# First-phase scaling of four projection jobs from SBUF, order pins for weight sums and statistics, and a later broadcast, in a fp32 decoder-block kernel

## The chip, the cores and the metric

The kernel runs on one core of a Trainium2 chip. The metric is the device time of one execution in microseconds (us), the median of several runs. TensorE (PE in the profile) multiplies matrices, VectorE (DVE) and ScalarE (ACT) work elementwise, GpSimd (POOL) does some elementwise work and issues DMAs, and SyncE (SP) issues DMAs.

## The reference

One layer over 2048 prompt tokens and 64 sample tokens, in fp32:

```
z = rms_norm(x, pre_g)
xr, gr, u, v, gs = split(z @ w_in)            # 1024 columns each
xc = causal_depthwise_conv(xr, buf, conv_w)   # 4 taps
hr = rg_lru(xc, sigmoid gates from w_r, w_i)  # recurrence along the tokens
br = hr * silu(gr)
bs = chunk_spatial_gating(gelu(u), rms_norm(gelu(v), sgu_g)) * silu(gs)
out = concat(br, bs) @ w_out
y = x + rms_norm(out, post_g)
```

rms_norm divides a token's row by the root of its mean square and multiplies by a gain for each channel.

## The kernel before, in words

**Groups and phases.** The tokens are cut into four groups of 512 prompt tokens; group 0 also takes the 64 sample tokens (T0 = 576 columns, two halves of 288). Phase one does group 0, and there a scheduler with priorities orders each engine's instructions. Phase two does groups 1 to 3 with Strassen-like products in steps, in the order in which the code is written (`manual_schedule`). Products keep fp32 precision by three matmuls, high times high, high times low and low times high.

**Weights.** A weight piece of 128x1024 is loaded by an SP DMA (`wraw`), ScalarE rounds it to a high half (`wh`, L187), VectorE subtracts that for the low half (`wl`, L195), and TensorE uses both. The work is prepared three pieces ahead, and a `wh` buffer comes free when TensorE has finished the piece three before.

**Jobs of phase one.** Jobs are 128 columns of w_in or w_out: xr0, xr1, gr8, gr9, xr2, xr3, gr10, gr11 and so on, then v, then gs, gs, u, u four times, then 16 out jobs. Here f0 to f3 are the first four. All but the v jobs have two pieces, 96 matmuls of 128x288 in all, and leave their result in two PSUM banks. The pool for them has six banks, so a job needs the banks of the job three before it. The matmuls run on x times gain. The division by the row norm comes after: `scaled` (L397) multiplies the two banks by rsB, a 128x576 tile with each token's factor. It is made by `norm_a` (`row_rstd`, L264: matmuls nsA and nsB sum the squares, VectorE takes the root's reciprocal) and `norm_b` (`row_bcast`, L289: VectorE builds the diagonal dg, matmuls nsC and nsD spread it over the partitions, VectorE copies it out). The same pair with the name "o" serves the norm after the out jobs, early in phase two (steps 4 and 10 of it), and `finish0` scales, adds and stores the 16 blocks of the result of group 0.

**Side work.** `make_sums` (L239) prepares weight sums for phase two: for each of 16 c-units (pairs of columns of w_in) POOL's queue loads four quadrants (B11, B12, B22, B21), VectorE adds four times, and POOL's queue stores the sums. For 12 more units (w_v, w_or) GpSimd does the adds. `stat_sum` and `z_norm` prepare group 1 during the out jobs. `later` keeps an instruction at its place in the program where the scheduler would otherwise issue it earlier by priority.

**Gates.** The xr jobs are scaled and convolved (`conv`, xc), split into xch and xcl, and multiplied with gate weights on TensorE (two spare banks), then go through sigmoids on ScalarE and a scan on VectorE. The first gate matmuls come behind the fifth job.

Of the kernel before, what the change touches and what calls it, by code (L numbers as in the profile page):

```python
# [11 lines left out]
AF = mybir.ActivationFunctionType  # L12
ALU = mybir.AluOpType
# [27 lines left out]
C_PRE, C_POST, C_CW, C_CB, C_BR, C_BI, C_LAM, C_SG = 0, 16, 32, 64, 72, 80, 88, 96  # L41
# [13 lines left out]
def hybrid_layer(ctx: ExitStack, tc: tile.TileContext, a):  # L55
    nc = tc.nc
# [15 lines left out]
    def blk(name, dt=F32):  # L72
        return bp.tile([P, T0 + 3], dt, tag="blk", name=name)
# [70 lines left out]
    state = {}  # L144
# [94 lines left out]
    def make_sums(unit):  # L239
        nm = "_".join(str(x) for x in unit)  # L240
        t = state.pop(("quad", unit))

        def put(k, x):
            sums[unit, k] = hp.tile([P, W], F32, name=f"{k}_{nm}")
            side.dma_start(sums[unit, k], x)

        eng = nc.vector if unit[0] == "c" else nc.gpsimd
        eng.tensor_add(t["B11"], t["B11"], t["B12"])
        put("P1", t["B11"])
        eng.tensor_add(t["B12"], t["B12"], t["B22"])  # L250
        put("P3", t["B12"])
        eng.tensor_add(t["B22"], t["B22"], t["B11"])
        put("P2", t["B22"])
        eng.tensor_add(t["B21"], t["B21"], t["B22"])
        put("P4", t["B21"])
# [98 lines left out]
    def banks(job):  # L354
        if ("ps", job) not in state:
            n = NC0 if is_v(job) else 2
            state["ps", job] = [bank(f"gm0{job[0]}{job[1]}_{o}") for o in range(n)]
        return state["ps", job]
# [35 lines left out]
    def cm_banks(job):  # L394
        return [(p[:, :n], o, n) for p, (o, n) in zip(banks(job), halves0)]

    def scaled(job, dst):  # L397
        rb = state["rxB"]
        for p, o, n in cm_banks(job):
            nc.vector.tensor_mul(dst[:, o:o + n], p, rb[:, o:o + n])  # L400

# [221 lines left out]
    def stat_sum(g, n):  # L623
        c, b = divmod(n, 2)
        if n == 0:
            state["xss", g] = mp.tile([P, 4, 2], F32, tag="xss", name=f"xss{g}")
        x = state.pop(("xs", g, n))
        nc.scalar.activation(x, x, AF.Square, accum_out=state["xss", g][:, c, b:b + 1])

    def stat_rstd(g):  # L630
        sv = mp.tile([P, 4], F32, tag="xsv", name=f"xsv{g}")
# [21 lines left out]
    def z_norm(g, j, rows=(0, 1)):  # L653
        x = state["R", g, j]
        for i in rows:
            nc.vector.scalar_tensor_tensor(x[:, i, :TP], x[:, i, :TP], col(C_PRE, 2 * j + i), state["rB", g],
                                           op0=ALU.mult, op1=ALU.mult)

    def parts(key, j):
        lo, hi = state[(*key, j)], state.get((*key, 4 + j))  # L660
# [84 lines left out]
    early, tasks, late = defaultdict(list), defaultdict(list), defaultdict(list)  # L745

    def at2(s, f, *args):

        tasks[s].append((f, *args))
# [300 lines left out]
    jobs = []  # L1050
# [8 lines left out]
    for job in jobs:  # L1059
        kind, j = job  # L1060
# [9 lines left out]
    for s in steps:  # L1070
        for job, i in s:
            kind, j = job
# [30 lines left out]
    handlers = {"xr": on_xr, "gr": on_silu, "gs": on_silu, "v": on_v0, "u": on_u0, "out": on_out0}  # L1103
    mid = {}
    plan = {job: [(handlers[job[0]], job)] for job in jobs}
# [1 line left out]
    def at(job, f, *args):  # L1107
        plan[job].append((f, *args))

    f0, f1, f2 = jobs[:3]  # L1110
    plan[f0], plan[f1] = [], []
    plan[f2] = [(norm_a, "x")]
    mid[jobs[3]] = [(norm_b, "x")] + [(handlers[f[0]], f) for f in (f0, f1, f2)] + [(gate_in0, 0), (gate_in0, 1)]
    for hp_ in range(0, NH, 2):
        i = jobs.index(("gr", NH + hp_ + 1))
        if hp_ == 0:
# [26 lines left out]
    for j in range(8):  # L1143
        at(("out", 8 + j // 2), z_raw, 1, j)
        at(("out", 11 + j // 3), z_norm, 1, j)
# [58 lines left out]
    for g in range(1, NG):  # L1204
        G = len(steps2)
        V, U, O, R2 = G + 56, G + 84, G + 140, G + 168
# [22 lines left out]
        wide(g, "v", "w_v", 0, put_v(g))  # L1229
        if g == 1:  # L1230
            for j in range(KT):
                t = 12 + 2 * j if j < 8 else V + 3 + 2 * (j - 8)
                at2(t, finish0_load, j)
                t += 3
                at2(t, finish0_scale, j)
                at2(t + 1, finish0_add, j)
                at2(t + 4, finish0_store, j)
        else:
            at2(G - 1, load_gq, g - 1, 1)
            for n in range(4):  # L1240
                k = (g - 1, (1, 1, 0, 0)[n], (3, 2, 2, 3)[n])
                t = G + (5, 7, 9, 11)[n]
                at2(t, finish_scale, *k)
                at2(t + 1, finish_add, *k)
                at2(t + 6, finish_store, *k)
            at2(V + 16, load_gq, g - 1, 0)
            for n in range(4):
                k = (g - 1, n % 2, n // 2)
                t = V + 21 + 3 * n
                at2(t - 5, finish_load, *k)  # L1250
                at2(t, finish_scale, *k)
                at2(t + 1, finish_add, *k)
                at2(t + 6, finish_store, *k)
# [70 lines left out]
    at2(R2 + 28, last_rstd, 0)  # L1324
    for qq in range(4):
        at2(R2 + 29, last_both, 0, qq)
    late[4].append((norm_a, "o"))
    late[10].append((norm_b, "o"))

    base = pos_of[steps2[0][3]]  # L1330
    with tc.manual_schedule():
# [84 lines left out]
```

## Time and profile before

| | |
|---|---|
| median of 3 runs | 2570.75 us (2570.57 to 2571.52) |
| profiled execution | 2568.9 us |
| its span | 2567.1 us |
| TensorE busy | 2497.7 us, 97% of the span |
| VectorE, ScalarE, POOL busy | 68%, 54%, 18% |
| mean granted TensorE clock | 0.991 of full speed |

The profile is of one execution, and 1.8 us of its time lie outside the span. A row of the timeline names an instruction and, in brackets, how long its engine had been idle before it and which instruction ended that. Line numbers in rows are those of the kernel before.

### The profile page before, as it was taken

What the parts mean: (1) busy time and instruction counts of PE and PEld (TensorE: products, weight loads), DVE (VectorE), ACT (ScalarE), POOL (GpSimd) and SP (SyncE); (2) the same over time, 40 slices, a digit from 0 to 9 for tenths busy, and PEclk for the clock granted to TensorE, in tenths of its full rate; (3) what the DMA queues carried; (4) which work ended last, traced back from release to release, by engine and by line L of the source; (5) the groups of instructions that cost most, each with busy time, mean ns of one, the idle gap of its engine ahead of it and who ended that gap; (6) DMA issues with size and microseconds to landing.
All of it is one profiled execution on the core that took longest, in us unless ns stands there. A gap on an engine that the chain in (4) does not pass through costs nothing.

```text
span 2567.1 us, 41558 instructions
## 1 busy us (share of the span) xinstructions
PE 2497.7 (97%) x16710; PEld 2300.2 (90%) x16710; DVE 1748.8 (68%) x2244; ACT 1391.6 (54%) x1777; POOL 470.5 (18%) x548
## 2 busy tenths in 40 slices
PE   7989999999999999999999999999999999999997
PEld 6989789999999998799878998799878998799886
DVE  7776155545466686756888686756888687756866
ACT  5444342223324577545756677545756577645654
POOL 4331024964751201100100100100000100100000
PEclk9999999999999999999999999999999999999999
DMA  6995389985964766756776755855776755855576
GB/s 226 332 328 214 107 286 322 369 276 193 323 221 155 228 210 207 233 182 187 268 260 197 239 192 180 252 178 186 258 274 197 240 177 185 254 192 181 187 253 198
DMA packets 167649, 587.11 MB, mean 229 GB/s; under 512 B 19216, under 2 KB 19776, under 8 KB 167456
## 3 DMA queue, kind: packets, MB, share of 16 engines
q1 hardware_dynamic: 107184, 378.11, 44.5%
q0 software_dynamic: 59696, 205.30, 24.0%
q8 instruction: 130, 2.13, 0.3%
q10 hardware_dynamic: 576, 1.05, 0.1%
q14 instruction: 63, 0.52, 0.1%
HBM read 494.92 MB, written 89.47 MB: 228 GB/s over the span
## 4 chain that ended last, share of the span: by engine, by line
PE 77%; DMA 7%; DVE 7%; ACT 5%; issue 3%; POOL 1%; SPq 0%; DVEq 0%; ACTq 0%; POOLq 0%
PE gm0out L370 8%; PE gm0v L381 4%; PE gm0gs L370 4%; PE gm0u L370 4%; PE gm0gr L370 3%; DMA wraw_c_P<-P_c 2%; PE gm0xr L370 2%; DVE wl_c_B L195 1%; DMA wraw_c_B<-w_in 1%; PE g L862 1%; PE sp L559 1%; PE w2o1a L716 1%; PE w2o1d L716 1%; PE w3o0d L716 1%; PE w1o1a L716 1%
## 5 line engine op out<-in xcount | busy, mean ns | idle before, releaser
L187 ACT ACTIVATE wh_c_P<-wraw_c_P 128x1024 fp32r<-128x1024 f32 x192 | 203.0, 1059 | 255.4 <-DMA wraw_c_P<-P_c 73.8
L195 DVE TENSOR_TENSOR wl_c_P<-wraw_c_P,wh_c_P 128x1024 fp32r<-128x1024 f32 x192 | 234.3, 1221 | 105.4 <-ACT wh_c_P L187 103.2
L195 DVE TENSOR_TENSOR wl_c_B<-wraw_c_B,wh_c_B 128x1024 fp32r<-128x1024 f32 x144 | 175.4, 1221 | 86.0 <-ACT wh_c_B L187 85.9
L187 ACT ACTIVATE wh_c_B<-wraw_c_B 128x1024 fp32r<-128x1024 f32 x144 | 152.2, 1058 | 147.6 <-DMA wraw_c_B<-w_in 24.8
L187 ACT ACTIVATE wh_w_or_P<-wraw_w_or_P 128x1024 fp32r<-128x1024 f32 x96 | 101.6, 1058 | 83.9 <-DMA wraw_w_or_P<-P_w_or 27.7
L195 DVE TENSOR_TENSOR wl_w_or_P<-wraw_w_or_P,wh_w_or_P 128x1024 fp32r<-128x1024 f32 x96 | 117.4, 1223 | 40.9 <-ACT wh_w_or_P L187 40.4
L187 ACT ACTIVATE wh_w_or_B<-wraw_w_or_B 128x1024 fp32r<-128x1024 f32 x72 | 76.1, 1059 | 79.6 <-DMA wraw_w_or_B<-w_or 15.8
L370 PE MATMUL gm0out<-c0l,wh_out 128*128 128x288 f32 x512 | 110.5, 297 | 1.0 <-DVE c0l L161 0.8
L370 PE MATMUL gm0out<-c0h,wh_out 128*128 128x288 f32 x512 | 110.7, 297 | 0.0
L370 PE MATMUL gm0out<-c0h,wl_out 128*128 128x288 f32 x512 | 110.1, 296 | 0.0
L195 DVE TENSOR_TENSOR wl_w_or_B<-wraw_w_or_B,wh_w_or_B 128x1024 fp32r<-128x1024 f32 x72 | 87.9, 1221 | 30.0 <-ACT wh_w_or_B L187 29.5
L195 DVE TENSOR_TENSOR wl_out<-wraw_out,wh_out 128x1024 fp32r<-128x1024 f32 x32 | 53.0, 1657 | 54.0 <-ACT wh_out L187 53.9
L620 POOL DMA_DIRECT2D xs<-xt x24 | 12.9, 538 | 391.5 <-PE sp L559 291.9
L370 PEld LDWEIGHTS gm0out<-c0l,wh_out 128*128 128x128 f32 x512 | 82.0, 188 | 1.6 <-DVE c0l L161 1.4
L431 POOL DMA_DIRECT2D wg<-w_g x16 | 11.9, 743 | 387.9 <-ACT xch L846 128.9
L370 PEld LDWEIGHTS gm0out<-c0h,wh_out 128*128 128x128 f32 x512 | 82.0, 188 | 0.6 <-issue 0.5
L370 PEld LDWEIGHTS gm0out<-c0h,wl_out 128*128 128x128 f32 x512 | 82.2, 188 | 0.0
L187 ACT ACTIVATE wh_out<-wraw_out 128x1024 fp32r<-128x1024 f32 x32 | 33.8, 1056 | 83.4 <-PE gm0out L370 51.6
L195 DVE TENSOR_TENSOR wl_w_v_P<-wraw_w_v_P,wh_w_v_P 128x1024 fp32r<-128x1024 f32 x48 | 58.5, 1221 | 29.6 <-ACT wh_w_v_P L187 29.6
L187 ACT ACTIVATE wh_w_v_P<-wraw_w_v_P 128x1024 fp32r<-128x1024 f32 x48 | 50.0, 1054 | 48.7 <-DMA wraw_w_v_P<-P_w_v 32.7
L370 PE MATMUL gm0gr<-z0h,wl_gr 128*128 128x288 f32 x256 | 57.3, 305 | 8.3 <-DVE wl_gr L195 8.3
L370 PE MATMUL gm0xr<-z0h,wh_xr 128*128 128x288 f32 x256 | 56.6, 303 | 7.2 <-ACT wh_xr L187 5.4
(1609 smaller groups left out, 8660.9 us busy)
## 6 DMA issues: line engine op xcount, KB each, us to landing
wraw_c_P<-P_c SPq DMA_DIRECT2D x192, 512.0 KB, 4.2
wraw_c_B<-w_in SPq DMA_DIRECT2D x144, 512.0 KB, 4.3
wraw_w_or_P<-P_w_or SPq DMA_DIRECT2D x96, 512.0 KB, 4.3
wraw_w_or_B<-w_or SPq DMA_DIRECT2D x72, 512.0 KB, 3.8
wraw_w_v_P<-P_w_v SPq DMA_DIRECT2D x48, 512.0 KB, 3.6
wraw_w_v_B<-w_v SPq DMA_DIRECT2D x36, 512.0 KB, 3.5
wraw_out<-w_out SPq DMA_DIRECT2D x32, 512.0 KB, 4.5
xs<-xt POOLq DMA_DIRECT2D x24, 512.0 KB, 5.8
```

Of the source, the lines that this page charges most:

```text
L187: nc.scalar.activation(h[:, sl], raw[:, sl], AF.Copy)
L195: nc.vector.tensor_sub(l[:, sl], raw[:, sl], h[:, sl].bitcast(F32))
L370: nc.tensor.matmul(p[:, :n], w, zz[:, o:o + n], start=(k == 0 and n_pass == 0), stop=(k == KT - 1 and n_pass == 2))
L381: nc.tensor.matmul(p[:n], zz[:, c * P:c * P + n], w, start=(k == 0 and n_pass == 0), stop=(k == KT - 1 and n_pass == 2))
L431: side.dma_start(w2.rearrange("p (h c) -> p h c", h=2), a["w_g"][hp_:hp_ + 2].rearrange("h p a c -> p h (a c)"))
L559: nc.tensor.matmul(p[:, c * P:(c + 1) * P], state["vn", c, h // 4][:, vs], wst[:, h, :], start=True, stop=True)
L620: side.dma_start(x, a[f"xt{g}"][c * P:(c + 1) * P, b * W:(b + 1) * W])
L716: nc.tensor.matmul(bks[b], zz, w, start=(not cont and kk == 0 and n_pass == 0), stop=(kk == HALF - 1 and n_pass == 2), skip_group_check=True)
L862: nc.tensor.matmul(p, ww[:, ws], xx[:, i, :TP], start=n_pass == 0, stop=n_pass == 2)
```

## The change

The first add of each c-unit, the squares of group 1's statistic and the first row of each of its `z_norm` blocks are pinned with `later`. A function `raw_out` copies both banks of f0 to f3 to an SBUF tile, and `scaled` multiplies that tile by rsB in one instruction of 576 columns. `norm_b("x")` moves from behind f3's first piece in the program to behind its second. `norm_a("o")` and `norm_b("o")` move from behind steps 4 and 10 of phase two to behind steps 8 and 14, and the `finish0` blocks shift: seven blocks from step 14 on, then the other nine from one step behind the start of the v products on.

```diff
@@ make_sums
-        eng.tensor_add(t["B11"], t["B11"], t["B12"])
+        i = eng.tensor_add(t["B11"], t["B11"], t["B12"])
+        if unit[0] == "c":
+            later(i)
@@
+    def raw_out(job):
+
+        t = state["rawp", job] = blk(f"raw0{job[0]}{job[1]}")
+        for p, o, n in cm_banks(job):
+            nc.vector.tensor_copy(t[:, o:o + n], p)
+
     def scaled(job, dst):
         rb = state["rxB"]
+        if ("rawp", job) in state:
+            nc.vector.tensor_mul(dst[:, :T0], state.pop(("rawp", job))[:, :T0], rb)
+            return
         for p, o, n in cm_banks(job):
             nc.vector.tensor_mul(dst[:, o:o + n], p, rb[:, o:o + n])
@@ stat_sum
-        nc.scalar.activation(x, x, AF.Square, accum_out=state["xss", g][:, c, b:b + 1])
+        i = nc.scalar.activation(x, x, AF.Square, accum_out=state["xss", g][:, c, b:b + 1])
+        if g == 1:
+            later(i)
@@ z_norm
+            if g == 1 and i == 0:
+                later(n)
@@
-    f0, f1, f2 = jobs[:3]
-    plan[f0], plan[f1] = [], []
-    plan[f2] = [(norm_a, "x")]
-    mid[jobs[3]] = [(norm_b, "x")] + [(handlers[f[0]], f) for f in (f0, f1, f2)] + [(gate_in0, 0), (gate_in0, 1)]
+    f0, f1, f2, f3 = jobs[:4]
+    plan[f0], plan[f1] = [], [(raw_out, f0), (raw_out, f1)]
+    plan[f2] = [(norm_a, "x"), (raw_out, f2)]
+    plan[f3] = ([(raw_out, f3), (norm_b, "x")] + [(handlers[f[0]], f) for f in (f0, f1, f2)]
+                + [(gate_in0, 0), (gate_in0, 1)] + plan[f3])
@@ finish0, the steps of phase two
-                t = 12 + 2 * j if j < 8 else V + 3 + 2 * (j - 8)
+                t = 14 + 2 * j if j < 7 else V + 1 + 2 * (j - 7)
@@
-    late[4].append((norm_a, "o"))
-    late[10].append((norm_b, "o"))
+    late[8].append((norm_a, "o"))
+    late[14].append((norm_b, "o"))
```

TensorE's order at the norm of x, in the kernel before (gm0gr_..._533 is f2, gm0gr_..._664 is f3):

```order
L370 MATMUL gm0gr_0_533<-z0h_271,wl_gr_1_477 128x288
L370 MATMUL gm0gr_1_534<-z0h_271,wl_gr_1_477 128x288
L272 MATMUL nsAx_641<-accx_121,ones 128x512
L276 MATMUL nsBx_644<-accx_121,ones 64x64
L296 MATMUL nsCx_715<-dgx_640,ones 128x512
L302 MATMUL nsDx_719<-dgx_640,ones 128x64
L370 MATMUL gm0gr_0_664<-z0h_117,wh_gr_0_529 128x288
L370 MATMUL gm0gr_0_664<-z0l_118,wh_gr_0_529 128x288
```

The same place in the changed kernel (gm0gr_0_673 is f3):

```order
L372 MATMUL gm0gr_1_540<-z0h_271,wl_gr_1_477 128x288
L274 MATMUL nsAx_647<-accx_121,ones 128x512
L278 MATMUL nsBx_650<-accx_121,ones 64x64
L372 MATMUL gm0gr_0_673<-z0h_117,wh_gr_0_535 128x288
L372 MATMUL gm0gr_1_674<-z0h_117,wh_gr_0_535 128x288
```

Here nsC and nsD no longer stand behind nsA and nsB. They stand behind the last matmul of f3, ahead of the fifth job (gm0xr_0_856):

```order
L372 MATMUL gm0gr_1_674<-z0l_272,wh_gr_1_591 128x288
L372 MATMUL gm0gr_0_673<-z0h_271,wl_gr_1_593 128x288
L372 MATMUL gm0gr_1_674<-z0h_271,wl_gr_1_593 128x288
L298 MATMUL nsCx_781<-dgx_646,ones 128x512
L304 MATMUL nsDx_785<-dgx_646,ones 128x64
L372 MATMUL gm0xr_0_856<-z0h_117,wh_xr_0_669 128x288
L372 MATMUL gm0xr_1_857<-z0h_117,wh_xr_0_669 128x288
```

So nsC and nsD have moved past all 96 matmuls of f3. On VectorE, in the first recurrence (heads 0 and 1: r, a and q are its factors), the order before is:

```order
L484 SCALAR_TENSOR_TENSOR r_0_952<-q_0_1168,r_0_952 128x576
L490 MEMSET a_0_1162 128x1
L497 MEMSET a_0_1162 128x8
L248 TENSOR_TENSOR pB11c_0_1900<-pB11c_0_1900,pB12c_0_1902 128x1024
L484 SCALAR_TENSOR_TENSOR r_1_974<-q_1_1172,r_1_974 128x576
L490 MEMSET a_1_1165 128x1
L497 MEMSET a_1_1165 128x8
L250 TENSOR_TENSOR pB12c_0_1902<-pB12c_0_1902,pB22c_0_1904 128x1024
L489 MEMSET r_0_952 128x1
L489 MEMSET r_1_974 128x1
L252 TENSOR_TENSOR pB22c_0_1904<-pB22c_0_1904,pB11c_0_1900 128x1024
L491 TENSOR_TENSOR i_0_963<-i_0_963,r_0_952 128x576
```

and in the changed kernel:

```order
L495 SCALAR_TENSOR_TENSOR r_0_960<-q_0_1176,r_0_960 128x576
L501 MEMSET a_0_1170 128x1
L508 MEMSET a_0_1170 128x8
L495 SCALAR_TENSOR_TENSOR r_1_982<-q_1_1180,r_1_982 128x576
L501 MEMSET a_1_1173 128x1
L508 MEMSET a_1_1173 128x8
L500 MEMSET r_0_960 128x1
L502 TENSOR_TENSOR i_0_971<-i_0_971,r_0_960 128x576
L500 MEMSET r_1_982 128x1
L507 TENSOR_TENSOR i_0_971<-i_0_971,ah_1189 128x8
L509 SCALAR_TENSOR_TENSOR xc_0_791<-a_0_1170,i_0_971 128x512
```

The adds of a c-unit (pB11c, pB12c, pB22c), which stood between the factors of the two heads, are gone from this stretch, and the next `wl_gr` stands 15 rows behind the first of the two r instead of 23. The second recurrence, heads 2 and 3, has lost its first adds in the same way. The adds come later: of the 16 units six instead of ten begin ahead of the v jobs, and the last one begins some 20 VectorE rows later among the gs and u jobs.

## Rows read from the trace of the kernel before

**Rows 1.** The page's first part: busy time of each engine, its share of the span, its instructions.

```profile
PE 2497.7 (97%) x16710; PEld 2300.2 (90%) x16710; DVE 1748.8 (68%) x2244; ACT 1391.6 (54%) x1777; POOL 470.5 (18%) x548
```

**Rows 2.** TensorE's waits, grouped (what waited, for whom, total us, times, longest us).

```profile
PE gm0gr L370 <- DVE wl_gr L195: 8.3, 2, 4.8
...
PE nsCx L296 <- DVE dgx L294: 5.2, 1, 5.2
...
PE nsCo L296 <- DVE dgo L294: 2.5, 1, 2.5
```

**Rows 3.** Timeline of TensorE over the statistics of the first norm and the fourth job. Columns here and in the other timelines: start us, duration us, engine, line, operation, out<-in, count, and in brackets the idle time just before and what ended it.

```profile
56.45 1.02 PE L272 MATMUL nsAx<-accx,ones 128*128 128x512 f32 x2
57.40 0.33 PE L276 MATMUL nsBx<-accx,ones 128*64 128x64 f32 x2
62.98 2.05 PE L296 MATMUL nsCx<-dgx,ones 128*128 128x512 f32 x2 [5.25 <-DVE dgx L294]
...
66.62 0.58 PE L370 MATMUL gm0gr<-z0h,wh_gr 128*128 128x288 f32 x1 [0.98 <-DVE xr L400]
...
81.58 0.43 PE L370 MATMUL gm0xr<-z0h,wh_xr 128*128 128x288 f32 x2
```

**Rows 4.** Timeline of TensorE at its two waits for a lower half of a gr weight.

```profile
134.37 0.53 PE L370 MATMUL gm0gr<-z0h,wl_gr 128*128 128x288 f32 x2 [3.51 <-DVE wl_gr L195]
...
181.59 0.85 PE L370 MATMUL gm0gr<-z0h,wl_gr 128*128 128x288 f32 x2 [4.78 <-DVE wl_gr L195]
182.23 0.68 PE L370 MATMUL gm0gr<-z0h,wh_gr 128*128 128x288 f32 x2
...
187.44 0.42 PE L370 MATMUL gm0gr<-z0h,wl_gr 128*128 128x288 f32 x2
187.70 0.42 PE L370 MATMUL gm0gr<-z0h,wh_gr 128*128 128x288 f32 x2
```

**Rows 5.** Timeline of VectorE ahead of those two waits.

```profile
123.91 1.23 DVE L248 TENSOR_TENSOR pB11c<-pB11c,pB12c 128x1024 f32<-128x1024 f32 x1 [4.28 <-DMA pB12c<-w_in]
...
133.11 1.20 DVE L195 TENSOR_TENSOR wl_gr<-wraw_gr,wh_gr 128x1024 fp32r<-128x1024 f32 x1
...
174.96 1.23 DVE L248 TENSOR_TENSOR pB11c<-pB11c,pB12c 128x1024 f32<-128x1024 f32 x1 [3.09 <-DMA pB12c<-w_in]
...
180.32 1.22 DVE L195 TENSOR_TENSOR wl_gr<-wraw_gr,wh_gr 128x1024 fp32r<-128x1024 f32 x1
```

**Rows 6.** Timeline of TensorE over the broadcast of the output norm, in the second phase.

```profile
832.94 2.05 PE L296 MATMUL nsCo<-dgo,ones 128*128 128x512 f32 x2 [2.54 <-DVE dgo L294]
835.93 0.69 PE L302 MATMUL nsDo<-dgo,ones 64*128 64x64 f32 x2 [0.94 <-DVE dgo L300]
836.54 0.79 PE L702 MATMUL q1xg0c<-R1D,wh_c_P 128*128 128x256 f32 x2
...
839.27 0.41 PE L702 MATMUL q1xg0c<-R1D,wh_c_P 128*128 128x256 f32 x2
...
839.99 0.40 PE L702 MATMUL q1xg0c<-R1D,wh_c_P 128*128 128x256 f32 x2
```

**Rows 7.** Timeline of VectorE at the same place.

```profile
832.11 0.68 DVE L294 TENSOR_TENSOR dgo<-ident,rsTo 128x512 f32<-128x512 f32 x1
835.03 0.69 DVE L298 COPY rsBo<-nsCo 128x512 f32<-128x512 f32 x1 [2.23 <-PE nsCo L296]
835.64 0.23 DVE L300 TENSOR_SCALAR dgo<-ident,rsTo 64x64 f32<-64x64 f32 x1
...
847.57 1.23 DVE L195 TENSOR_TENSOR wl_c_P<-wraw_c_P,wh_c_P 128x1024 fp32r<-128x1024 f32 x1 [0.27 <-ACT wh_c_P L187]
```

**Rows 8.** Stretches after the second weight wait and after the broadcast: start:end, length, busy time of PE, PEld, DVE, ACT, POOL (with instructions), granted TensorE clock, DMA share, GB/s.

```profile
181.60:187.40 5.80, 5.80 (x24) 5.80 (x25) 5.80 (x16) 2.21 (x3) 2.80 (x6) 0.51 0.97 325
836.50:839.30 2.80, 2.80 (x14) 2.76 (x14) 1.96 (x3) 0.00 (x0) 0.00 (x0) 0.50 0.00 0
```

**Rows 9.** VectorE's instructions by line and shape: count, busy us, mean ns of one, and the idle time before them with what ended it.

```profile
L248 DVE TENSOR_TENSOR pB11c<-pB11c,pB12c 128x1024 f32<-128x1024 f32 x16 | 19.5, 1221 | 36.1 <-DMA pB12c<-w_in 36.0
...
L594 DVE COPY o<-gm0out 128x288 f32<-128x288 f32 x32 | 13.1, 451 | 31.3 <-PE gm0out L370 31.3
...
L505 DVE TENSOR_TENSOR xc<-xc,gr 128x576 f32<-128x576 f32 x8 | 5.9, 743 | 0.0
```

**Rows 10.** Timeline of VectorE (one row from before the statistics, three from the chain that scales and convolves the first jobs) and of TensorE at the first gate matmul.

```profile
57.47 1.22 DVE L195 TENSOR_TENSOR wl_xr<-wraw_xr,wh_xr 128x1024 fp32r<-128x1024 f32 x1 [4.89 <-PE nsAx L272]
...
66.03 0.81 DVE L400 TENSOR_TENSOR xr<-gm0xr,rsBx 128x288 f32<-128x288 f32 x2
...
75.28 0.75 DVE L161 TENSOR_TENSOR xcl<-xc,xch 128x576 fp32r<-128x576 f32 x1
...
94.38 0.29 PE L460 MATMUL gr<-xch,wgh 128*128 128x288 f32 x1
```

**Rows 11.** Timelines of POOL and of VectorE in one stretch where GpSimd adds weight quadrants.

```profile
452.25 2.40 POOL L250 TENSOR_TENSOR pB12w_v<-pB12w_v,pB22w_v 128x1024 f32<-128x1024 f32 x1
...
452.56 3.19 DVE L195 TENSOR_TENSOR wl_u<-wraw_u,wh_u 128x1024 fp32r<-128x1024 f32 x1 [0.18 <-ACT wh_u L187]
```

**Rows 12.** Timeline of POOL where the quadrant sums end and the branch results are read back for the out jobs.

```profile
556.94 0.57 POOL L245 DMA_DIRECT2D P_w_or<-pB21w_or  x1 [0.30 <-POOL pB21w_or L254]
...
590.26 3.23 POOL L343 DMA_DIRECT2D cb<-cat  x6
```

More of the change, by code (lines that the diff above doesn't have):

```diff
@@ L655, in z_norm @@
         for i in rows:
-            nc.vector.scalar_tensor_tensor(x[:, i, :TP], x[:, i, :TP], col(C_PRE, 2 * j + i), state["rB", g],
-                                           op0=ALU.mult, op1=ALU.mult)
+            n = nc.vector.scalar_tensor_tensor(x[:, i, :TP], x[:, i, :TP], col(C_PRE, 2 * j + i), state["rB", g],
+                                               op0=ALU.mult, op1=ALU.mult)
+            if g == 1 and i == 0:
+                later(n)
     def parts(key, j):
```

## The prediction

> **What bounds the kernel now.** I read the page's engine shares first, then the grouped waits of TensorE, then the timelines of TensorE and VectorE around each wait that the change touches, then the granted clock there. TensorE is busy for 97% of the span [rows 1], so time can be won only where it waits or runs at the lower clock. Of its waits, three groups touch what the change moves: the lower halves of two gr weights (8.3 us in two waits), nsC of the first norm (5.2 us) and nsC of the output norm (2.5 us) [rows 2]. The reader is to see that each costs more than its bracket, because matmuls behind a wait can run at 1.2 GHz instead of 2.4 for a while: the granted clock is 0.51 of full in the 5.8 us behind the second weight wait and 0.50 in the 2.8 us behind the broadcast [rows 8].
>
> **The change part by part.** All sums are against the profiled execution, 2568.9 us.
>
> *Raw banks and the later nsC of x.* TensorE has finished nsB at 62.98 - 5.25 = 57.73, and the fifth job starts at 81.58 [rows 3]. These 23.85 us hold nsC, nsD and f3. The wait for VectorE's chain, matmuls at twice their full-clock duration (nsC 2.05 us where the equal nsA takes 1.02), the 0.98 us wait for f0's banks and slow matmuls of f3 all lie in them. In the changed order f3 follows nsB at once, and its banks are free because f0 was copied out long before. A job takes 94.38 - 81.58 = 12.80 us at full clock (the fifth job, from its first matmul to the first gate matmul [rows 3, 10]). nsC and nsD at the pace of nsA and nsB take 57.73 - 56.45 = 1.28 us [rows 3]. 12.80 + 1.28 = 14.08, so the term is 23.85 - 14.08 = **9.77 us**. The statistic chain on VectorE then has a whole job of 12.8 us for what took 5.25 us.
>
> What it adds: eight copies of 128x288 from PSUM and four SBUF multiplies of 128x576 in place of eight PSUM multiplies. The copy is shown elsewhere at 451 ns and a 576-column product of two SBUF tiles at 743 ns [rows 9]. A PSUM multiply takes about 0.81 / 2 = 0.41 us, from the pair at 66.03 [rows 10]. VectorE's extra work is 8 x 0.451 + 4 x 0.743 - 8 x 0.41 = 3.3 us. The copies stand where VectorE idled (4.89 us ahead of 57.47 [rows 10]), so I count them as nothing. Were that cover gone, 3.3 us would be the upper bound of the loss. A gain from the edit itself is excluded, because the work only grows.
>
> Against this edit stands the Trainium skill, "VectorE: DVE Perf Modes", section "Rules for kernel authors": take an elementwise operation on a matmul's result straight from PSUM at the lower rate, and copy to SBUF first only where many operations follow. Here one multiply follows, so by that rule the edit only adds the 3.3 us. The rows agree on the added work, but put it where VectorE waited; the rule does not price the bank that the copy frees.
>
> Where is the next late thing? Scaling and convolution of heads 0 and 1 now start after nsC, at about 57.73 + 12.80 + 1.28 = 71.8, plus a weight subtraction of 1.2 us and the copies of rsB that stand ahead of the multiplies on VectorE (some 0.9 us, estimated from nsC's copy of 0.69 and a shorter one beside it [rows 7]): 73.9. Before, the stretch from the first multiply (66.03) to the end of head 0's xcl (76.03) took 10.0 us with one c-unit add of 1.2 us in it [rows 9, 10], so I estimate xcl at 73.9 + 8.8 = 82.7, against first gate matmuls at 71.8 + 12.8 = 84.6. The slack falls from 18.4 us (94.38 - 76.03) to about 2 us. I take the stall as 0. Its upper bound is that of the worst weight wait below, 7.4 us.
>
> *Pins on the c-unit adds.* In both recurrences VectorE stood at the first add of a c-unit, waiting 4.28 and 3.09 us for the quadrant's DMA [rows 5]. The next wl_gr, queued behind it on the same engine, came at 133.11 and 180.32, and TensorE waited 3.51 and 4.78 us for these two [rows 4, 5]. After the second wait twelve pairs of matmuls run from 181.59 to 187.44 instead of at the full-clock pitch 187.70 - 187.44 = 0.26 to 0.27: 5.85 - 12 x 0.267 = 2.65 us of lower clock [rows 4]. (The first wait shows none: its first pair takes 0.53 us and not 0.85.) With the adds gone from both stretches VectorE gives back 4.28 and 3.09 us of waiting and three adds of 1.22 us in the first, two in the second [rows 5, 9]: 7.9 and 5.5 us against the 3.51 and 4.78 needed. Term: 3.51 + 4.78 + 2.65 = **10.94 us**. Lower bound 0: the adds still wait for DMAs in total 36.0 us over 16 units [rows 9], and where a pinned add waits ahead of another weight piece the stall reappears. More than the wait and its clock can't be won there.
>
> *The output norm's broadcast.* TensorE stops at 832.94 - 2.54 = 830.40 and resumes at 836.54, 6.14 us [rows 6]. Steps 8 and 14 give VectorE time to work off its queue: at the new place it waits for ScalarE's weight halves itself (0.27 us ahead of 847.57 [rows 7]). nsC at full clock is 1.02 us, nsD 0.33 [rows 3]. The 0.94 us ahead of nsD stays: in this manual order the copy of nsC (835.03) stands ahead of the second part of dgo (835.64) on VectorE, and nsD needs that part [rows 6, 7]. 1.02 + 0.94 + 0.33 = 2.29 remain, 3.85 go. Behind it four groups of three matmuls took 839.27 - 836.54 = 2.73 us where two groups at full clock took 839.99 - 839.27 = 0.72, so 1.44 for four: 1.29 us of lower clock. The term is 3.85 + 1.29 = **5.1 us** if the shorter pause leaves the clock up. Lower bound: 0, if VectorE is just as late there. The new dgo comes right behind the subtraction that in before ends at 847.57 + 1.23 = 848.80; + 0.68 = 849.5, which is about when TensorE ends the piece. That is tight, so a few tenths may stay.
>
> *The rest.* The finish0 shift moves DMAs on POOL's queue by some steps and one scaling instruction into the v products; the squares and z_norm pins move work within the out jobs, where VectorE waits for TensorE (31.3 us ahead of the copies of the out banks [rows 9]). I take 0. The bound is two weight waits as above, 8.3 us [rows 2], lost or nothing gained. SP's loads keep their order. POOL's later quadrant work ends at 556.94 and the last read-back for the out jobs is issued at 590.26 [rows 12]. With TensorE 9.77 + 10.94 = 20.7 us earlier, that read is due at 569.6, still 12.1 us behind POOL's end if POOL's work does not move at all. So nothing is given back there.
>
> Sum: 9.77 + 10.94 + 5.1 = 25.8. 2568.9 - 25.8 = 2543.1 in a profiled execution. The median of the runs lies 2570.75 - 2568.9 = 1.85 above it, so I predict **2545.0 us**.
>
> **The rivals.**
> *The stall only moves.* The pinned adds still wait 36 us for their quadrants, somewhere. If two such waits meet a weight that is due, as they did before, the 10.94 us come back: 2545 + 10.9 = 2556. For it: VectorE works strictly in order. Against: the new places lie behind a weight subtraction and outside the dense recurrence.
>
> *The scaling chain is late.* The gates' slack is 2 us by my estimate. A stall as the second weight wait, 4.78 + 2.65 = 7.4, gives 2552. For it: a 16 us loss of slack. Against: the chain lost its add.
>
> *Slower: VectorE's adds beside GpSimd's.* Four c-units more than before begin behind the v jobs, towards the stretch in which GpSimd adds. Beside such an add of 2.40 us a VectorE subtraction took 3.19 us instead of 1.22 [rows 9, 11]. Four adds ahead of a weight then cost 4 x (3.19 - 1.22) = 7.9 us a unit. From 25.8 / 7.9 = 3.3 units on, none of it hidden, the kernel is slower than before; with seven of the ten late units it takes 2545 + 55 = 2600. Against: only the last units reach that stretch, and three pieces of weights are prepared ahead. The Trainium skill, "GPSIMD Engine Reference", in its table of specifications, says that GpSimd shares SBUF interfaces with VectorE and collides with instructions of two SBUF inputs, which both subtraction and adds are; the 3.19 us agree with it.
>
> **How the numbers follow.** Forecast 0.68, with its own range 2541 to 2551 (the tight places add up to 6 us, and 4 us below for waits that I left). Stall moved 0.14, late scaling 0.10, slower 0.08. The range 2540 to 2558 holds the forecast's and the two middle cases, and leaves out the slower one and some tails of the others. A measurement of this kernel tells 0.2% (5.1 us) from no change: below 2565.6 is faster. The first three cases lie there: 0.90 with a little off for tails. Same 0.03, slower 0.07.
>
> **What would show it.** Right: the two waits for wl_gr and the one for nsC of x are gone, TensorE runs unbroken from the start of f3 to the gates at about 84.6, no L248 wait stands inside a recurrence, and the pause at the output norm is about 2.3 us at full clock. Wrong: a wait of gr (L460) for xcl or xch near 84 (late scaling); new waits for wl of xr, v, gs or u behind an L248 row with a DMA bracket (stall moved); VectorE subtractions of 3 us and more in front of waiting u jobs, with c-unit adds beside them (slower).

## The result

The changed kernel takes 2546.06 us (median of 4 runs, 2542.83 to 2553.36) against 2570.66 us (4 runs, 2566.87 to 2571.52). The ratio is 0.9905, with a 95% interval of 0.9878 to 0.9931. The prediction was 2545.0 us, 2540 to 2558.

The span of the profiled execution fell from 2567.1 to 2545.4 us. The page's first part of the changed kernel (busy time, share and instructions, as [rows 1]):

```profile
PE 2489.8 (98%) x16710; PEld 2292.5 (90%) x16710; DVE 1766.6 (69%) x2248; ACT 1393.3 (55%) x1779; POOL 469.5 (18%) x548
```

TensorE has lost 7.9 us of busy time at the same number of matmuls (its mean granted clock rose from 0.991 to 0.996 of full speed), and the other 13.8 us of the span's difference were idle time.

**Where the time went.** The table divides TensorE's timeline at the first row that writes a named result and gives the length of each stage, in us, worked out from the start times in the traces. (gm0xr is the first job, nsAx the first norm's sum, gm0v the v jobs, gm0out the out jobs, nsx the spread of group 1's statistic, q1xg0a the start of phase two, q1xg2a its third xg product, w1va the v products, q1ug0a the u products of group 1.) The last row is all later stages together.

| stage | before | changed | difference |
|---|---|---|---|
| gm0xr start to nsAx | 51.08 | 50.86 | -0.22 |
| nsAx to gm0v | 202.24 | 181.38 | -20.86 |
| gm0v to gm0out | 329.40 | 329.43 | +0.03 |
| gm0out to nsx | 144.06 | 146.30 | +2.24 |
| nsx to q1xg0a | 64.85 | 64.84 | -0.01 |
| q1xg0a to q1xg2a | 93.86 | 87.21 | -6.65 |
| q1xg2a to w1va | 86.73 | 86.96 | +0.23 |
| w1va to q1ug0a | 89.90 | 92.66 | +2.76 |
| q1ug0a to the end | 1499.61 | 1500.44 | +0.83 |

Nearly all of the gain lies where the statistics of x and the recurrences are (predicted 9.77 + 10.94 = 20.71) and around the output norm. Two stages give some back.

TensorE at the first norm, the rows that answer to [rows 3] and to the gate of [rows 10]:

```profile
57.13 0.33 PE L278 MATMUL nsBx<-accx,ones 128*64 128x64 f32 x2
...
70.30 1.02 PE L298 MATMUL nsCx<-dgx,ones 128*128 128x512 f32 x2
71.26 0.43 PE L304 MATMUL nsDx<-dgx,ones 64*128 64x64 f32 x2
71.62 0.53 PE L372 MATMUL gm0xr<-z0h,wh_xr 128*128 128x288 f32 x2
...
84.51 0.30 PE L471 MATMUL gr<-xch,wgh 128*128 128x288 f32 x1
```

nsC has no bracket, and TensorE runs at the full-clock duration of 1.02 us where it took 2.05. From the end of nsB (57.13 + 0.33 = 57.46) to the fifth job are 14.16 us, against 23.85 before and 14.08 predicted. VectorE over the same stretch, and at the two weights of [rows 5] (rows at 113.91 and 161.24; the one at 121.09 is the next c-unit's first add):

```profile
56.25 0.82 DVE L403 COPY raw0gr<-gm0gr 128x288 f32<-128x288 f32 x2 [4.22 <-PE gm0gr L372]
...
62.49 0.24 DVE L302 TENSOR_SCALAR dgx<-ident,rsTx 64x64 f32<-64x64 f32 x1
...
70.37 0.82 DVE L403 COPY raw0gr<-gm0gr 128x288 f32<-128x288 f32 x2 [4.17 <-PE gm0gr L372]
...
72.52 0.68 DVE L300 COPY rsBx<-nsCx 128x512 f32<-128x512 f32 x1
...
80.95 0.75 DVE L161 TENSOR_TENSOR xcl<-xc,xch 128x576 fp32r<-128x576 f32 x1
...
113.91 1.22 DVE L195 TENSOR_TENSOR wl_gr<-wraw_gr,wh_gr 128x1024 fp32r<-128x1024 f32 x1
...
121.09 1.22 DVE L248 TENSOR_TENSOR pB11c<-pB11c,pB12c 128x1024 f32<-128x1024 f32 x1
...
161.24 1.22 DVE L195 TENSOR_TENSOR wl_gr<-wraw_gr,wh_gr 128x1024 fp32r<-128x1024 f32 x1
```

The copies (L403, from PSUM to SBUF) stand directly behind an idle time of 4.22 and 4.17 us. The second half of dgx is written at 62.49, long before nsC at 70.30. rsB is copied from 72.52 on, and head 0's xcl ends at 80.95 + 0.75 = 81.70, 2.8 us ahead of its gate matmul at 84.51. Both `wl_gr` have no bracket, and the c-unit add at 121.09 stands behind the recurrence and doesn't wait. Nor does any other of the 16 first adds, which waited 36.0 us in all before [rows 9]. The same group in the changed kernel (count, busy us, mean ns of one, idle us before them):

```profile
L248 DVE TENSOR_TENSOR pB11c<-pB11c,pB12c 128x1024 f32<-128x1024 f32 x16 | 19.5, 1216 | 0.0
```

By the time VectorE comes to the pinned adds, their quadrants have landed.

At the output norm, TensorE and then VectorE, as [rows 6, 7]:

```profile
821.86 1.10 PE L298 MATMUL nsCo<-dgo,ones 128*128 128x512 f32 x2 [0.24 <-DVE dgo L296]
823.89 0.43 PE L304 MATMUL nsDo<-dgo,ones 64*128 64x64 f32 x2 [0.94 <-DVE dgo L302]
824.26 0.50 PE L717 MATMUL q1xg1a<-R1A,wh_c_B 128*128 128x256 f32 x2
```

```profile
819.89 1.23 DVE L195 TENSOR_TENSOR wl_c_P<-wraw_c_P,wh_c_P 128x1024 fp32r<-128x1024 f32 x1 [0.28 <-ACT wh_c_P L187]
821.03 0.68 DVE L296 TENSOR_TENSOR dgo<-ident,rsTo 128x512 f32<-128x512 f32 x1
823.00 0.69 DVE L300 COPY rsBo<-nsCo 128x512 f32<-128x512 f32 x1 [1.28 <-PE nsCo L298]
823.60 0.24 DVE L302 TENSOR_SCALAR dgo<-ident,rsTo 64x64 f32<-64x64 f32 x1
```

A wait of 0.24 us is left for nsC (VectorE's dgo stands right behind a weight subtraction), and the 0.94 us ahead of nsD is there as before, since its part of dgo still stands behind the copy of nsC. From 821.62 to 824.26 TensorE loses 2.64 us where it lost 6.14.

### The profile page after: what moved, and what is told of

Same layout as the page of the kernel before. It is cut to its first block, busy times and chain, and to the rows that moved or that the text cites. A ratio compares the mean times of both kernels' runs of the same rounds, so it can differ in the third digit from the quotient of the medians.

```text
span 2545.4 us, 41569 instructions
## 1 busy us (share of the span) xinstructions
PE 2489.8 (98%) x16710; PEld 2292.5 (90%) x16710; DVE 1766.6 (69%) x2248; ACT 1393.3 (55%) x1779; POOL 469.5 (18%) x548
## 4 chain that ended last, share of the span: by engine, by line
PE 73%; DMA 8%; DVE 6%; ACT 5%; POOL 4%; issue 4%; SPq 0%; DVEq 0%; ACTq 0%; POOLq 0%
PE gm0out L372 8%; PE gm0v L383 4%; PE gm0gr L372 4%; PE gm0xr L372 3%; DMA wraw_c_B<-w_in 2%; DMA wraw_w_v_P<-P_w_v 1%; DVE wl_c_B L195 1%; PE g L877 1%; PE gm0gs L372 1%; DMA wraw_w_v_B<-w_v 1%; PE w2o0d L731 1%; PE w1o0d L731 1%; PE w2o1a L731 1%; PE w3o0d L731 1%; PE w2o1d L731 1%
## 5 line engine op out<-in xcount | busy, mean ns | idle before, releaser
L187 ACT ACTIVATE wh_w_or_B<-wraw_w_or_B 128x1024 fp32r<-128x1024 f32 x72 | 76.1, 1058 | 80.4 <-DMA wraw_w_or_B<-w_or 20.5
L383 PE MATMUL gm0v<-wh_v,z0l 128*128 128x512 f32 (+1 forms) x160 | 63.2, 396 | 0.0
L383 PE MATMUL gm0v<-wl_v,z0h 128*128 128x512 f32 (+1 forms) x160 | 63.1, 395 | 0.0
```

The source lines that it names most:

```text
L187: nc.scalar.activation(h[:, sl], raw[:, sl], AF.Copy)
L383: nc.tensor.matmul(p[:n], zz[:, c * P:c * P + n], w, start=(k == 0 and n_pass == 0), stop=(k == KT - 1 and n_pass == 2))
```

## The experiments

Runs of one kernel spread over 4 to 18 us here, so each verdict rests on the ratio to the kernel before on the same chip and on the stage lengths, which come from one trace of each kernel. (The kernel before had a median of 2569.11 us beside e1 to e4, 2570.00 beside e5 to e8 and 2570.07 beside e9 to e11; its row in the table is that of the result.) Stage R repeats within 0.01 us in the five traces with the pinned adds, the later broadcast and the old spacing of the units. Where the adds are not pinned it repeats only within 1 us: 202.24 and 201.27 (before and e3) and 196.56 and 195.70 (e2 and e4) are pairs whose edits do not differ in this stage. "Stage R" is nsAx to gm0v, "stage S" gm0out to nsx, "stage X" q1xg0a to q1xg2a, "stage V" w1va to q1ug0a, "stage U" q1ug0a to the first w_or product (165.44 before, 165.31 in the changed kernel).

| run | median us | ratio, 95% interval | R | S | X | V |
|---|---|---|---|---|---|---|
| before | 2570.66 | | 202.24 | 144.06 | 93.86 | 89.90 |
| changed kernel | 2546.06 | 0.9905 (0.9878 to 0.9931) | 181.38 | 146.30 | 87.21 | 92.66 |
| e1 unit pins only | 2561.89 | 0.9973 (0.9960 to 0.9987) | 190.87 | 143.94 | 95.35 | 90.16 |
| e2 raw banks only | 2563.32 | 0.9972 (0.9958 to 0.9985) | 196.56 | 143.72 | 96.31 | 90.01 |
| e3 output norm only | 2565.60 | 0.9984 (0.9970 to 0.9999) | 201.27 | 144.08 | 86.96 | 93.27 |
| e4 all but unit pins | 2557.61 | 0.9954 (0.9939 to 0.9970) | 195.70 | 144.23 | 89.94 | 92.62 |
| e5 finish0 as before | 2549.56 | 0.9927 (0.9907 to 0.9947) | 181.37 | 146.93 | 91.50 | 90.33 |
| e6 broadcast half a job later | 2548.00 | 0.9917 (0.9894 to 0.9941) | 181.40 | 143.68 | 87.41 | 93.02 |
| e7 no statistic pins | 2546.25 | 0.9914 (0.9891 to 0.9936) | 181.38 | 145.35 | 86.70 | 93.35 |
| e8 finish0 eleven steps later | 2547.60 | 0.9917 (0.9894 to 0.9939) | 181.37 | 146.71 | 86.62 | 87.01 |
| e9 units 19.5 us apart | 2559.14 | 0.9955 (0.9938 to 0.9972) | 189.01 | 149.78 | 87.10 | 93.49 |
| e10 finish0 seven steps later | 2543.96 | 0.9899 (0.9877 to 0.9921) | 181.37 | 145.06 | 87.18 | 88.64 |
| e11 e6, e9 and e10 together | 2560.64 | 0.9961 (0.9947 to 0.9975) | 188.47 | 149.48 | 89.16 | 88.88 |

**e1, the pins alone.** The edit to the kernel before:

```diff
-        eng.tensor_add(t["B11"], t["B11"], t["B12"])
+        i = eng.tensor_add(t["B11"], t["B11"], t["B12"])
+        if unit[0] == "c":
+            later(i)
```

> The kernel before with the pin on the first add of each c-unit, and nothing else of the change. Theory (each edit pays at its own place): the two waits for wl_gr (3.51 and 4.78 us, with 2.65 us of lower clock) go, about 1.3 us come back at the spatial product ahead of the out jobs because POOL's work slips, 2570.7 - 10.9 + 1.3 = 2561 us. Rival (the stall only moves to the weights behind which the pinned adds now stand): 2569 to 2571, with waits of 3 to 5 us for other wl pieces.

Measured: 2561.89 us, and stage R is 11.37 us shorter (10.94 expected). TensorE has no wait of 0.6 us or more for a weight between the fourth job and the out jobs. The rival falls: the pinned adds wait for no quadrant here either (0.0 us over all 16), and cost no other weight piece anything. The median fell by only 7.2 us against that of before on the same chip (by the interval 3 to 10); in the trace the stages behind q1ug0a, which the pins do not touch, are 2.4 us longer. The return at the spatial product that the theory expected here did not come (stage S 143.94), which e9 takes up.

**e2, the raw banks alone.** The kernel before with `raw_out`, the two-way `scaled` and the plan of the first four jobs as in the change, and nothing else.

> The kernel before with the raw copies of the first four jobs' banks and the broadcast of x behind the fourth job, and nothing else. Theory: nsC of x no longer waits, 2570.7 - 9.8 = 2561 us; the two waits for wl_gr stay (8.3 us in all) since the adds are still free to move. Rival (the place of the x statistics is what pushed the adds into the recurrences): these waits go too, 2550 us.

Measured: 2563.32 us, stage R 5.68 us shorter, neither of the two. The waits stay, but both have come together in the second recurrence, and both are followed by the lower clock (pairs of 0.85 us, as at 181.59 in [rows 4]). TensorE and VectorE there:

```profile
169.71 0.85 PE L370 MATMUL gm0gr<-z0h,wh_gr 128*128 128x288 f32 x2 [5.90 <-ACT wh_gr L187]
...
176.55 0.85 PE L370 MATMUL gm0gr<-z0h,wl_gr 128*128 128x288 f32 x2 [5.52 <-DVE wl_gr L195]
```

```profile
163.99 1.23 DVE L248 TENSOR_TENSOR pB11c<-pB11c,pB12c 128x1024 f32<-128x1024 f32 x1 [6.94 <-DMA pB12c<-w_in]
...
175.30 1.20 DVE L195 TENSOR_TENSOR wl_gr<-wraw_gr,wh_gr 128x1024 fp32r<-128x1024 f32 x1
```

The first wait of before (3.51 us without loss of clock) is gone. In its place VectorE waits 6.94 us for a quadrant in one piece, which delays two weights. So the x statistics did not cause the waits, but they set where they fall.

**e4, everything but the unit pins.** The changed kernel without the edit of e1.

> The changed kernel without the pin on the c-unit adds. Theory: the two waits in the recurrences are back, POOL's slip is gone: 2546 + 10.9 - 1.3 = 2556 us. Rival (with the earlier x statistics the adds land elsewhere by themselves, the pin adds nothing): 2545 us.

Measured: 2557.61 us, 11.6 us over the changed kernel's median (12.6 by the two ratios), and stage R is 14.32 us longer (195.70 - 181.38), with the same two waits in the second recurrence (4.35 and 5.51 us). So the pin is worth 11.4 us alone and 14.3 us beside the raw banks. The raw banks are worth 5.7 us alone (e2) and 190.87 - 181.38 = 9.5 us beside the pins, which is the 9.77 of the prediction. The two edits do not add up singly: 5.7 + 11.4 = 17.1, together 20.9.

**e3, the output norm's later steps and the finish0 shift alone.**

> The kernel before with norm_a and norm_b of the output norm four steps later and the finish0 shift, and nothing else. Theory: 5.1 to 6.0 us go at the broadcast and 2 to 3 us come back at the start of the v products, where one finish0 block more now stands, 2567 to 2568 us. Rival (the finish0 shift costs nothing, the v products' waits vary by themselves): 2565 us.

Measured: 2565.60 us, on the rival's number. But on this chip the kernel before took 2569.11, not the 2570.66 of the result. The drop of 3.5 us is the theory's (2.7 to 3.7 from 2570.66) rather than the rival's (5.7), though the interval (0.3 to 7.7 us) holds both. The stages speak for the theory: X is 6.90 us shorter and V 3.37 us longer.

**e5, finish0 at its old steps.** The edit to the changed kernel:

```diff
-                t = 14 + 2 * j if j < 7 else V + 1 + 2 * (j - 7)
+                t = 12 + 2 * j if j < 8 else V + 3 + 2 * (j - 8)
```

> The changed kernel with the finish0 blocks at their steps of before (the first of them is scaled at step 15, behind the broadcast at step 14, so nothing else has to move). Theory (the finish0 shift is what the start of the v products pays for): the stage from the first v product to the first u product is 90 us as before instead of 92.7, so 2543 us; TensorE's waits for w_v weights fall from 8 to about 6 us. Rival (those waits come from VectorE's recurrence and the output norm, whatever finish0 does): 92.7 us in that stage, 2546 us.

Measured: 2549.56 us, neither of the two. Stage V is back at 90.33, and the waits for w_v weights fall from 7.0 to 5.3 us, as the theory says. What I had not expected is stage X: 91.50, 4.29 us longer than with the shift. The nsC wait is as in the changed kernel, but the next xg product waits for its weight, and the matmuls behind it run at the lower clock (0.58 us, 0.39 at the same place in the changed kernel):

```profile
866.76 0.58 PE L717 MATMUL q1xg1d<-R1F,wl_c_B 128*128 128x256 f32 x1 [4.08 <-DVE wl_c_B L195]
```

The same wait is 2.01 us before and 1.52 us in the changed kernel. ScalarE stands ahead of it, in e5 and then in the changed kernel, at a sigmoid of the gates (its result i takes a buffer of the pool that the finish0 blocks, fo, use), until the store of such a block has ended:

```profile
856.09 1.27 ACT L883 ACTIVATE i<-g,cv 128x512 f32<-128x512 f32 x2 [5.63 <-DMA y<-fo]
```

```profile
851.95 1.26 ACT L883 ACTIVATE i<-g,cv 128x512 f32<-128x512 f32 x2 [2.66 <-DMA y<-fo]
```

Over the traces TensorE's wait grows with this idle time: 0.96 us behind 1.47 (e7), 1.52 behind 2.66 (changed kernel), 2.01 behind 3.18 (before), 2.57 behind 3.73 (e4), 4.09 behind 5.31 (e2) and 4.08 behind 5.63 (e5). With finish0 at its old steps the idle time is 3.18 to 5.63 us, with the shift 1.47 to 3.73. So the shift is no bystander, but e5 lies at the upper end, and one trace does not give the shift's own share of the 4.29 us. Besides, 1.44 us of it come back in the next stage (q1xg2a to w1va 85.52 against 86.96), and 2.33 in stage V: from q1xg0a to q1ug0a e5 takes 267.35 us and the changed kernel 266.83. Later norm steps with the old finish0 shorten stage X by 2.36 us only, in this trace.

**e6, the broadcast half a job later instead of a whole one.** `norm_b("x")` goes behind f3's first piece, the rest of the plan stays:

```diff
-    plan[f3] = ([(raw_out, f3), (norm_b, "x")] + [(handlers[f[0]], f) for f in (f0, f1, f2)]
+    mid[f3] = [(norm_b, "x")]
+    plan[f3] = ([(raw_out, f3)] + [(handlers[f[0]], f) for f in (f0, f1, f2)]
```

> The changed kernel with the broadcast of x behind the first piece of the fourth job instead of the second, 6.4 us behind nsB instead of 12.8. Theory (VectorE's chain takes about 5.5 us from nsA on, any later place is enough): no wait for nsC over 0.3 us, 2546 us, and xcl is ready about 6 us earlier. Rival (the whole job is needed, because copies and weights stand in the chain's way): nsC waits 1 to 5 us, part of the following matmuls run at 1.2 GHz, 2548 to 2555 us.

Measured: 2548.00 us, stage R 181.40, the same. TensorE and VectorE:

```profile
59.52 0.33 PE L278 MATMUL nsBx<-accx,ones 128*64 128x64 f32 x2
...
66.55 1.02 PE L298 MATMUL nsCx<-dgx,ones 128*128 128x512 f32 x2
```

```profile
68.50 0.68 DVE L300 COPY rsBx<-nsCx 128x512 f32<-128x512 f32 x1
...
74.16 0.82 DVE L403 COPY raw0gr<-gm0gr 128x288 f32<-128x288 f32 x2 [4.84 <-PE gm0gr L372]
74.91 0.75 DVE L408 TENSOR_TENSOR xr<-raw0xr,rsBx 128x576 f32<-128x576 f32 x1
```

nsC has no bracket, so half a job is enough for VectorE's chain. The earlier xcl did not come: rsB is copied at 68.50, but f3's copies stand ahead of the first multiply on VectorE and wait for f3's end at 74.16. In a strict order an earlier factor alone moves nothing.

**e7, without the statistic pins.**

> The changed kernel without the pins on the squares and on z_norm of group 1. Theory: no effect, 2546 us, every stage within 0.5 us of the changed kernel's. Rival (the squares, unpinned, go ahead of the out jobs' work on ScalarE): some us more or less between the first out matmul and the statistic's spread.

Measured: 2546.25 us; stages R, X and V within 0.7 us, stage S 0.95 us shorter, which is more than the 0.5 us that the theory had allowed. The pins on the squares and z_norm do not show in the time. One trace can't tell whether the part in stage S is theirs, since that stage varies with POOL (below).

**e8 and e10, finish0 elsewhere in the v products.** `V + 1` becomes `V + 12` and `V + 8`.

> The changed kernel with its last nine finish0 blocks eleven steps later, behind the dense start of the v products. Theory: the stage of the v products takes 89 us or less instead of 92.7 and nothing is paid later, since VectorE waits for weights there: 2542 us. Rival (the blocks only push the waits to the later v steps and the first u products): 2546 us.

> The changed kernel with the last nine finish0 blocks seven steps later, so that their scaling lies behind the last recurrence of the first xg stage and ends before the first u product. Theory: the v stage takes 88 us or less, the u stage 165.3 as in the changed kernel, 2542 us. Rival (VectorE is full until the u products, any place here costs): the two stages together take 258 us as in the changed kernel, 2546 us.

Measured: with eleven steps 2547.60 us: stage V falls to 87.01, but stage U rises from 165.31 to 169.51 (TensorE waits 2.44 us there for the lower half of a weight), as the rival says. With seven steps 2543.96 us (2542.41 to 2546.50): stage V 88.64, stage U 165.84, together 3.5 us less than in the changed kernel. The waits at the start of the v products, in the changed kernel and the VectorE rows ahead of the first:

```profile
996.13 0.50 PE L731 MATMUL w1vb<-wl_w_v_P,R1E 128*128 128x512 f32 x1 [1.08 <-DVE wl_w_v_P L195]
...
1000.99 0.50 PE L731 MATMUL w1vb<-wh_w_v_P,R1E 128*128 128x512 f32 x1 [2.02 <-ACT wh_w_v_P L187]
...
1007.72 0.50 PE L731 MATMUL w1vd<-wl_w_v_P,R1D 128*128 128x512 f32 x1 [1.00 <-DVE wl_w_v_P L195]
```

```profile
992.99 1.23 DVE L902 SCALAR_TENSOR_TENSOR t<-q,t 128x1024 f32<-128x1024 f32 x1 [2.52 <-ACT q L898]
994.13 0.81 DVE L617 SCALAR_TENSOR_TENSOR fo<-fo,cv,rsBo 128x576 f32<-128x576 f32 x1
994.86 1.22 DVE L195 TENSOR_TENSOR wl_w_v_P<-wraw_w_v_P,wh_w_v_P 128x1024 fp32r<-128x1024 f32 x1
```

and the same three VectorE instructions in e10:

```profile
990.70 1.22 DVE L902 SCALAR_TENSOR_TENSOR t<-q,t 128x1024 f32<-128x1024 f32 x1 [2.52 <-ACT q L898]
991.84 1.22 DVE L195 TENSOR_TENSOR wl_w_v_P<-wraw_w_v_P,wh_w_v_P 128x1024 fp32r<-128x1024 f32 x1
992.97 0.81 DVE L617 SCALAR_TENSOR_TENSOR fo<-fo,cv,rsBo 128x576 f32<-128x576 f32 x1
```

The finish0 scaling (L617) no longer stands between the recurrence's factor (L902) and the weight subtraction. This kernel has the lowest median of the study, but its ratio's interval (0.9877 to 0.9921) overlaps that of the changed kernel. The stages show the gain in V twice, since e11 with the same finish0 steps has 88.88. They do not show that U stays: in e11 it is 169.88. TensorE waits 2.80 us there for the lower half of a weight (1.36 in e10), behind ScalarE's wait for the DMA of a weight piece, 3.77 us against 1.70. V and U together are then 258.8, against 258.0 in the changed kernel. So the 3.5 us of e10 are not assured.

**e9 and e11, units planned closer.** `45 + 20.5 * n` and `64 + 20.5 * n` become `45 + 19.5 * n` and `64 + 19.5 * n`.

> The changed kernel with its 28 units of weight sums planned 19.5 us apart instead of 20.5, so that POOL ends its adds earlier before the out jobs. Theory (POOL's late end bunches the read-backs and puts four c0l subtractions ahead of s on VectorE): no wait of sp for s, the stage from the first out matmul to nsx takes 143.7 to 144.1 instead of 146.3, 2544 us. Rival (the wait comes from something else, or the denser units cost in the recurrences what they give here): 2546 us or more.

> The changed kernel with the unit spacing of 19.5, the finish0 blocks seven steps later and the broadcast of x behind the first piece of the fourth job. Theory: the parts add, 2546 - 2.2 - 4 - 0 = 2540 us. Rival: each only moves the next wait, 2545 us.

Measured: 2559.14 and 2560.64 us, far on the rival's side. In e9 TensorE waits for a gr weight of the third recurrence and for s:

```profile
230.54 0.85 PE L372 MATMUL gm0gr<-z0h,wl_gr 128*128 128x288 f32 x2 [4.80 <-DVE wl_gr L195]
...
582.83 2.07 PE L570 MATMUL sp<-wst,vn 128*128 128x128 f32 x8 [4.79 <-DVE s L576]
```

```profile
222.49 1.22 DVE L248 TENSOR_TENSOR pB11c<-pB11c,pB12c 128x1024 f32<-128x1024 f32 x1
...
224.28 1.22 DVE L252 TENSOR_TENSOR pB12c<-pB12c,pB22c 128x1024 f32<-128x1024 f32 x1
...
226.08 1.22 DVE L254 TENSOR_TENSOR pB22c<-pB22c,pB11c 128x1024 f32<-128x1024 f32 x1
...
227.88 1.22 DVE L256 TENSOR_TENSOR pB21c<-pB21c,pB22c 128x1024 f32<-128x1024 f32 x1
...
229.27 1.22 DVE L195 TENSOR_TENSOR wl_gr<-wraw_gr,wh_gr 128x1024 fp32r<-128x1024 f32 x1
```

With the closer plan four adds of a unit fall between the third recurrence and the next convolution, 4 x 1.22 us in front of `wl_gr`. In the first two recurrences the pins had taken such adds out; here the adds wait for no DMA, and their work alone is enough. And the wait for s grows to 4.79 us instead of going. (sp is the last spatial product on TensorE, into a PSUM bank; s is VectorE's reading of the bank of the product before.) What that wait hangs on is seen over all runs: how long before the first out matmul POOL issues the first read-back of the branch results (cb), against the wait of sp for s.

| run | cb ahead of gm0out, us | wait of sp for s, us |
|---|---|---|
| e2 | 23.54 | none |
| e4 | 23.52 | none |
| before | 23.28 | none |
| e3 | 23.27 | none |
| e6 | 15.13 | none |
| e1 | 14.44 | none |
| e10 | 14.21 | 0.19 |
| e7 | 14.07 | 0.50 |
| changed kernel | 13.45 | 1.34 |
| e5 | 12.97 | 2.29 |
| e8 | 12.96 | 2.66 |
| e11 | 10.65 | 4.54 |
| e9 | 10.16 | 4.79 |

The later cb, the longer the wait, from about 14.4 us on. POOL, VectorE and TensorE in the changed kernel:

```profile
439.73 0.53 POOL L237 DMA_DIRECT2D pB21w_v<-w_v  x1 [3.86 <-DMA P_c<-pB11c]
445.73 3.48 POOL L248 TENSOR_TENSOR pB11w_v<-pB11w_v,pB12w_v 128x1024 f32<-128x1024 f32 x1 [5.47 <-DMA pB12w_v<-w_v]
...
552.97 0.57 POOL L245 DMA_DIRECT2D P_w_or<-pB21w_or  x1 [0.30 <-POOL pB21w_or L256]
553.54 2.14 POOL L345 DMA_DIRECT2D cb<-cat  x4
```

```profile
565.12 2.76 DVE L161 TENSOR_TENSOR c0l<-cb,c0h 128x576 fp32r<-128x576 f32 x4
567.80 0.82 DVE L411 TENSOR_TENSOR u<-gm0u,rsBx 128x288 f32<-128x288 f32 x2
568.53 1.22 DVE L195 TENSOR_TENSOR wl_out<-wraw_out,wh_out 128x1024 fp32r<-128x1024 f32 x1
569.66 0.74 DVE L576 SCALAR_TENSOR_TENSOR s<-sp,cv,bsb 128x512 f32<-128x512 f32 x1
```

```profile
570.46 1.16 PE L570 MATMUL sp<-wst,vn 128*128 128x128 f32 x8 [1.34 <-DVE s L576]
```

POOL issues cb right behind the last store of its sums. On VectorE four c0l subtractions of these read-backs stand ahead of u, a weight and s. They do so in the kernel before as well, where s starts 0.86 us behind the first out matmul; here it starts 2.67 us behind it, and the product waits. POOL began its adds 19.4 us earlier than before (413.44 against 432.85) but ended them only 4.0 us earlier (552.97 against 556.94 in [rows 12]): among others it waited 3.86 us for a store of the last c-unit and 5.47 us for the quadrants that this held up. The closer plan did start the adds earlier: the first one in e9 stands at 409.62. It failed because it put a ninth unit ahead of the read-back: 36 of GpSimd's adds come before cb in e9 and e11, 32 in every other run, and in e9 cb is issued at 565.75. Beside this, e9 and e11 lost 7 to 8 us in stage R.

## Why the prediction was right

**The x statistics (9.77).** Right: 23.85 us became 14.16. The gates' slack, estimated at 2 us, was 2.8; the late-scaling rival did not occur. VectorE's added work is as estimated (eight copies in 3.44 us, four multiplies in 3.01, for eight multiplies of some 3.3), and no wait of TensorE comes of it. e6 shows that half of the delay suffices.

**The pins (10.94).** Right together with the raw banks: stage R fell by 20.86 against 20.71, and e1 gives 11.37 alone. The stall-moves rival is refuted by e1. Its premise, which the term's lower bound shares, was wrong: "The pinned adds still wait 36 us for their quadrants, somewhere." They wait 0.0 us, so there was no stall left to move. What the sum did not see is that the terms depend on each other: the raw banks alone would have won 5.7, because the unpinned adds then cost 3 to 4 us more (e2, e4). That the sum holds for the two together is right; for either edit without the other it would not have been the same.

**The output norm (5.1).** The step itself is right: 6.14 us became 2.64 (2.29 predicted, and the tenths that were called tight are there). Of the lower clock behind it 1.2 of the 1.29 us went: four groups of three matmuls take 1.51 us instead of 2.73. That is 4.7 of the 5.1. Stage X gained 6.65; the other 1.9 us are not of this term, and by e5 the finish0 shift has a part in them.

**The rest, taken as 0, was mis-sized in two places.** For finish0 the 0 came out nearly right, 0.5 us by e5, but as the sum of two effects that I had not seen: the v products lose 2.3 to 3.6 us (89.90 to 90.33 in the four traces with the old steps, 92.62 to 93.49 in the six with the change's own shift), and the xg products gain, 2.9 us in e5's comparison. That these nearly cancel is luck. My cover was VectorE's waiting in the out jobs, which is not where finish0 stands. "So nothing is given back there" for POOL should have been 1.3 us: I compared POOL's end with the last read-back, but the wait hangs on the first, and POOL's end moved up by 4 us while the out jobs moved up by 21. The size of this wait is partly chance: it is none to 2.66 us in the runs e5 to e8 and e10, none of which was to move POOL's adds. Of stage S's 2.24 us, 1.34 are that wait; the rest was not traced to one instruction.

**The slower rival** (adds beside GpSimd's) did not occur: the stage from gm0v to gm0out differs by 0.03 us, although nine units begin in it instead of six. Its sign on VectorE is there, subtractions for u weights of 3.02 and 3.41 us, but TensorE has no wait in the whole stage:

```profile
427.92 3.41 DVE L195 TENSOR_TENSOR wl_u<-wraw_u,wh_u 128x1024 fp32r<-128x1024 f32 x1
```

The sum of the profiled execution came out at 21.7 us of span against 25.8. Of the 4.1 us between, 5.0 are the returns in stages S and V, and 0.8 more the later stages, against 1.7 us won beyond the terms in stages R and X. The profiled execution took 2547.09 us where 2543.1 was forecast. That the median is nevertheless within 1.1 us of 2545 is partly chance: runs of the changed kernel spread over 10.5 us.

## What to carry to other kernels

On an engine that works strictly in order, an operation that waits for a DMA belongs behind the subtraction that TensorE needs next, not among the links of a dense chain; a pin was enough here, since by its new place the data had landed, and it was worth more once another change had moved the rest. It does not make the work free: in e9 four adds that wait for nothing still hold up a weight. A scaling factor that comes late need not hold PSUM banks: copy raw, scale later, and check what else then stands ahead of the first scaled result. After a gain on one engine, look at which neighbour's end did not move with it, and at its first consumer, not its last.

## What the runs showed of the hardware

- Not every stop lowered the granted clock, and the length of the stop did not decide it: behind the 3.51 us before the first weight it was 1.00 of full in the next 3 us [rows 4], behind the 2.54 us at the output norm 0.50 [rows 6]. Waits of 4.35 and 5.9 us in e4 and e2 were followed by pairs of 0.85 us, and the 4.08 us in e5 by matmuls of 0.58 instead of 0.39 us.
- Runs of one kernel spread over 4 to 18 us. In the traces the stage from the third group's u products to its first w_or product took 166.9 to 171.9 us, and the start up to nsAx 50.9 to 53.1 us, though no edit touched either.
